# Gate table of an expert layer: matmul outputs interleaved in PSUM, eviction read straight through

## The chip, the cores and the metric

The kernel runs on one NeuronCore of a Trainium2 chip. The core has a matrix engine (TensorE, PE in the profile; its weight loads have a row of their own, PEld), a vector engine (VectorE, DVE), a scalar engine (ScalarE, ACT), GpSimd (POOL), and SyncE (SP), whose queue here only starts DMA transfers. Matmuls write PSUM, a small memory of 128 partitions with eight banks of 512 float32 values in each; ScalarE or VectorE then copy ("evict") the result into the main on-chip memory, SBUF. The metric is the device time of one execution in microseconds, the median of several runs.

## What is computed

Two layers of a transformer trunk on 512 tokens of width 1024. Each layer is an attention part (four kinds of heads) and an expert part. The expert part is the one that matters here; cut down, it reads:

```
q = (h @ w_q) ; s1, s2 = scores of 128 + 128 sub-keys, per token and head
v1,i1 = top16(s1) ; v2,i2 = top16(s2)
top_s, top_j = top16 of the 256 sums v1 + v2
eid  = i1 * 128 + i2 of the chosen pairs        # 16 of 16384 experts per head, 8 heads
gate = softmax(top_s)
act  = gelu(h . u[eid]) ; out = sum over chosen experts of gate * act * v[eid]
```

The kernel does not gather experts for the first 384 tokens. It computes the activations of all 16384 experts for them, in 128 blocks of 128, and multiplies them by a dense table of gates that is zero where an expert was not chosen. The table has, for each of the 384 tokens, 128 x 128 gates (first sub-key x second sub-key). The last 128 tokens gather their experts.

## The kernel before

`peer` (one call per layer) builds the gate table in the middle of its first stage. The table of one token is a product of two one-hot matrices, one of them scaled by the gates: 128 partitions are the token's 128 (head, choice) pairs, so a matmul sums them up.

- The table is built in 48 batches `b` of 8 tokens. `g_ones(b)` (line 1632, VectorE) makes the one-hot arrays `o` in float16 for both sub-keys. `g_scale(b, q, eng)` makes `og`, the first one-hot times the gate: `q` = 0 is the high half of the gate, `q` = 1 the rest of it, so that two float16 products carry the gate's precision. Line 1646 is its form on VectorE (one instruction for 8 tokens), line 1644 its form on ScalarE (8 instructions, one per token).
- Each batch has two groups `j` of four tokens. `g_mm(j)` (line 1654) takes a PSUM bank (tag `a`, six banks) and runs 8 matmuls of 128 columns into it: four tokens `t`, each the sum of `q` = 0 and `q` = 1. Token `t` fills columns `t*128` to `t*128+127`.
- `g_out(j)` (line 1660, ScalarE) evicts the bank of 512 columns into `gs`, a tile of 128 partitions x 128 sub-keys `a` x 32 tokens. In `gs` the tokens are innermost, so for one token neighbouring sub-keys are 32 float32 (128 bytes) apart. The eviction reads the bank straight through (token by token) and its writes step by 128 bytes.
- Eight groups fill a `gs` tile (two buffers); `g_put` (line 1663) sends its 2 MB to `gdram` in HBM from SyncE's queue.

There are 96 groups per layer, 192 in all: 1536 matmuls of line 1654 and 192 evictions of line 1660.

Beside the table run the activations of expert blocks: `u_load` (line 1343, SyncE), `u_hi` (line 1347, ScalarE) and `u_lo` (line 1350, VectorE or GpSimd) split a block of 128 x 1024 weights into two parts, `u_mm` (lines 203 to 205, tag `b`) runs 24 matmuls of 384 columns on it, `u_act` (line 1363, ScalarE) applies the gelu. VectorE also decodes the choices of the last 128 tokens (lines 1544 to 1595).

What comes in which order on each engine is decided before the program is built: `Plan` takes steps with a due time and an estimated duration (0.49 us for `g_out`, 0.45 us for `g_mm`) and writes a fixed sequence for each engine. At the end of the stage four held `u_mm` blocks run. The next stage, a loop over 128 expert blocks (`prepare`, `products`), needs the whole table: it begins with three loads of `vr` (line 1797), a load of `gq` out of `gdram` (line 1802) and six gathers (line 1750), which reuse the memory of the table's tiles.

Of the kernel before, what the change touches and what calls it, by code (L numbers as in the profile page):

```python
# [16 lines left out]
AF = mybir.ActivationFunctionType  # L17
# [25 lines left out]
GSC = 2.0 ** 14  # L43
# [1283 lines left out]
def peer(nc, tc, I, l, xd, fh, fl, h3, closing, q0, w012, both, wq_mm, right, hp, up, small, bank, mm3, iota128, pos, ident, dram, grow, ada, more, rows_out):  # L1327
    V, S, G, PE, SY = nc.vector, nc.scalar, nc.gpsimd, nc.tensor, nc.sync
# [35 lines left out]
    with tc.tile_pool(name=f"Q{l}", bufs=1) as qp:  # L1364
# [18 lines left out]
        def ac(n):  # L1383
            return "S", 0.05 + n / 1090
# [5 lines left out]
        def wq_part(h, half, eng):  # L1390

            if h not in w:
                w[h] = [q[:, :, h % 2 * 256:h % 2 * 256 + 256] for q in both]
            for k in (4 * half, 4 * half + 2):
                ks = slice(k, k + 2)
                if eng is S:
                    S.activation(w[h][0][:, ks], raw[h][:, ks], AF.Copy)
                else:
                    eng.tensor_sub(w[h][1][:, ks], raw[h][:, ks], w[h][0][:, ks])
# [10 lines left out]
        def wq_out(h, c, t=slice(0, T)):  # L1410
            if h not in qcs:
                qcs[h] = wp.tile([128, 2, T], F32, name="qc", tag="qc", bufs=3)
            S.activation(qcs[h][:, c, t], (q0[2 * h + c] if h < 2 else q1[h, c])[:, t], AF.Copy)
# [61 lines left out]
        for h in range(8):  # L1475
            t0 = 10.2 * (h - 1)
            if h > 2:
                loads[h] = plan.add(t0 - 16, lambda h=h: wq_load(h), ("Q", 3.2), take=("wr",))
                wsplit[h] = []
                for half in range(2):  # L1480
                    a = plan.add(t0 - 7 + half, lambda h=h, half=half: wq_part(h, half, S), ("S", 1.0), after=(loads[h], wtake[h] if half else None), take=("w",) if half == 0 else ())
# [5 lines left out]
            for c in range(2):  # L1487
                if h < 2:
                    m0 = plan.add(-99, none, ("none", 0), take=("a",))
                    o = plan.add(WL[0] + c, lambda h=h, c=c: wq_out(h, c, slice(0, 256)), ac(256), after=(m0, *outs), take=("qc",) if c == 0 else ())  # L1490
                    m = plan.add(WL[1] + WL[2] * (2 * (1 - h) + c), lambda h=h, c=c: wq_late(h, c), ("PE", 2.6), after=(m0, m), give=(("w", wtake[1]),) if (h, c) == (1, 1) else ())
                    late.append(plan.add(WL[1] + WL[2] * (2 * (1 - h) + c) + 2, lambda h=h, c=c: wq_out(h, c, slice(256, 512)), ac(256), after=(m, o), give=(("a", m0),)))
                else:
                    m0 = plan.add(t0 + 5.1 * c, lambda h=h, c=c: wq_half(h, c, 0), ("PE", 2.56), after=(wsplit[h][0], m), take=("a",))
                    m = plan.add(t0 + 5.1 * c + 2.5, lambda h=h, c=c: wq_half(h, c, 1), ("PE", 2.56), after=(m0, wsplit[h][1]), give=(("w", wtake[h]),) if c else ())
                    o = plan.add(t0 + 5.1 * c + 5, lambda h=h, c=c: wq_out(h, c), ac(512), after=(m, *outs), take=("qc",) if c == 0 else (), give=(("a", m0),))
# [42 lines left out]
        if True:  # L1539
# [9 lines left out]
            def ids(i, q, eng):  # L1549

                c = cids[i, q] = wp.tile([128, NC2, 8], I16, name="cid", tag="cid", bufs=2)
                o = 0
                for k0, n, wd in SELB[q]:
                    shp = [128, n, wd, 8]
                    eng.tensor_tensor(out=c[:, o:o + n * wd].rearrange("p (a b) h -> p a b h", a=n), in0=bc(ifl[:, 1, i, None, 0:wd], shp),
                                      in1=bc(ifl[:, 0, i, k0:k0 + n, None], shp), op=ALU.add)
                    o += n * wd
# [67 lines left out]
            gst, gps, oo, gg = {}, {}, {}, {}  # L1625
# [22 lines left out]
            def g_mm(j):  # L1648
                b, g = divmod(j, 2)
                o, h = oo[b], gg[b]  # L1650
                gps[j] = bank("a")
                for t in range(4):
                    for q in range(2):
                        PE.matmul(gps[j][:, t * 128:(t + 1) * 128], lhsT=o[:, 2 * g + 1, :, t], rhs=h[:, q, g, :, t], start=q == 0, stop=q == 1)  # L1654

            def g_out(j):
                tg, t4 = divmod(j, TG // 4)
                if t4 == 0:
                    gst[tg] = dp.tile([128, 128, TG], F32, name="gs", tag="gs", bufs=GL[4])
                S.activation(gst[tg][:, :, 4 * t4:4 * t4 + 4].rearrange("p a t -> p t a"), gps.pop(j).rearrange("p (t a) -> p t a", t=4), AF.Copy, scale=1 / GSC)  # L1660

            def g_put(tg):
                SY.dma_start(gdram[tg], gst.pop(tg))
# [2 lines left out]
            turns, a, f = [], None, None  # L1666
            for i in range(NT):
# [4 lines left out]
                for q in range(4):  # L1672
                    a = plan.add(due + d * q, lambda e, i=i, q=q: ids(i, q, E[e]), [("G", 0.2 * len(SELB[q]) + NSEL[q] / 60), ("W", 0.08 * len(SELB[q]) + NSEL[q] / 240)],
                                 after=(head, a), take=("cid",))
# [12 lines left out]
            for b in range(NG // 2):  # L1687
                due, (ids_, gts) = B0 + GD[0] + GD[1] * b, turns[b // 16]
                one = plan.add(due, lambda b=b: g_ones(b), ("W", 1.135), after=(ids_,), take=("o",))
                hi = plan.add(due + 1, lambda e, b=b: g_scale(b, 0, E[e]), [("W", 0.602), ("S", 2.4)], after=(one, gts), take=("og",))  # L1690
                lo = plan.add(due + 1, lambda e, b=b: g_scale(b, 1, E[e]), [("W", 0.602), ("G", 2.3), ("S", 2.4)][:LA], after=(hi,))
                for j in (2 * b, 2 * b + 1):
                    give = (("o", one), ("og", hi)) if j % 2 else ()
                    m = plan.add(due + 2, lambda j=j: g_mm(j), ("PE", 0.45), after=(lo, m if j % 2 else None), take=("a",), give=give)
                    outs.append(plan.add(due + 3, lambda j=j: g_out(j), ("S", 0.49), after=(m, *outs[:1]), take=("gs",) if j % 8 == 0 else (), give=(("a", m),)))
                if b % 4 == 3:
                    plan.add(due + 3, lambda b=b: g_put(b // 4), ("Q", 6.5), after=outs, give=(("gs", outs[0]),))
                    outs = []
# [91 lines left out]
    with tc.tile_pool(name=f"D{l}", bufs=1) as dp, ExitStack() as order:  # L1790
# [136 lines left out]
        with tc.tile_pool(name=f"X{l}", bufs=1) as xp:  # L1927
# [6 lines left out]
            def evac(i):  # L1934
                if i < 3:
                    half_out(i, 0)
                    half_out(i, 1)
                if state is not None:
                    SY.dma_start(xd[i], xs[i])
                r = put(i, xs[i], xp)  # L1940
                if state is None:
                    return r
                r[0]()
                return r[1:]
# [11 lines left out]
            if state is None:  # L1956
                scale, rest = evac(3)
                for i in range(2):
# [4 lines left out]
                    scale, rest = nxt  # L1963
# [152 lines left out]
```

## Time and profile before

| | us |
|---|---|
| median of 3 runs | 3342.16 (3340.18 to 3348.39) |
| the profiled execution | 3341.59 |
| its span, first to last instruction | 3339.8 |
| PE busy in the span | 3183.5 (95%) |
| DVE busy | 2585.4 (77%) |
| ACT busy | 1516.9 (45%) |
| line 1660, 192 evictions | 194.9 on ACT, 1144 ns each |
| line 1654, 1536 matmuls | 204.2 on PE, 295 ns each from start to end |

The table stage lies at about 522 to 720 us for the first layer and 2171 to 2368 us for the second. "Busy" of PE counts a matmul from its start to the end of its last write, and neighbouring matmuls overlap; how fast they follow each other is read from the start of the first and the start of the next, or from a run of many of them. The same holds for ScalarE: an eviction's row says 1144 ns, but the next one starts before it has ended.

### The profile page before, as it was taken

To read this page: it belongs to the slowest core of one execution; us is meant where nothing else is said; L and a number is where in the kernel's file an instruction comes from. 1 tells how busy PE (TensorE), PEld (TensorE's weight loads), DVE (VectorE), ACT (ScalarE), POOL (GpSimd) and SP (SyncE) were. 2 spreads that over 40 slices of the span, in tenths; PEclk is the share of its full clock that TensorE was granted. 3 is DMA by queue.
4 is the path that set the end of the run, shared out by engine and by line. 5 is a ranking of instruction groups with operands and counts; after the bars stand their busy time and mean duration, and the time that the engine had idled before them with its cause. 6 is when DMAs were issued, how large, how long until landed. Compare 5 with 4: busy or idle time off the path is not lost.

```text
span 3339.8 us, 48260 instructions
## 1 busy us (share of the span) xinstructions
PE 3183.5 (95%) x17540; PEld 2816.0 (84%) x17540; DVE 2585.4 (77%) x5528; ACT 1516.9 (45%) x2763; POOL 851.9 (26%) x682
## 2 busy tenths in 40 slices
PE   6999999979999999999999999998899999999998
PEld 6876879869989999998888668897799899999987
DVE  7767798858878888786666868988578787878856
ACT  3267527873333333333432864289533333333333
POOL 1300210004433343341022002100234344444400
PEclk9999999869999999999999999997899999999999
DMA  8402304459889989896654032144688899999954
GB/s 281 145 9 95 128 33 152 177 217 334 324 323 336 347 322 335 323 352 232 201 177 142 1 133 103 51 163 184 255 316 328 311 336 321 326 325 325 323 183 163
DMA packets 291343, 762.77 MB, mean 228 GB/s; under 512 B 23832, under 2 KB 130968, under 8 KB 285984
## 3 DMA queue, kind: packets, MB, share of 16 engines
q1 hardware_dynamic: 217376, 491.22, 42.3%
q0 software_dynamic: 73728, 268.47, 21.8%
q8 instruction: 137, 2.24, 0.3%
q14 instruction: 102, 0.84, 0.1%
HBM read 700.86 MB, written 58.74 MB: 227 GB/s over the span
## 4 chain that ended last, share of the span: by engine, by line
PE 75%; DVE 11%; ACT 8%; DMA 4%; issue 2%; POOL 0%; SPq 0%; DVEq 0%; ACTq 0%; POOLq 0%
PE psa L204 12%; PE psa L205 12%; PE psa L203 12%; PE psb L203 10%; PE psb L205 9%; PE psb L204 9%; ACT gs L1660 3%; PE psa L1654 2%; ACT og L1644 2%; PE psa L863 2%; PE psa L896 1%; DMA gq<-gdram 1%; DVE s L1437 1%; DMA wr<-in_w_in 1%; ACT P L877 1%
## 5 line engine op out<-in xcount | busy, mean ns | idle before, releaser
L203 PE MATMUL psb<-bh,uh 128*128 128x384 f32 x2048 | 692.0, 338 | 3.0 <-ACT act L1363 1.2
L205 PE MATMUL psb<-bh,ul 128*128 128x384 f32 x2048 | 688.9, 336 | 3.0 <-DVE ul L1350 3.0
L204 PE MATMUL psb<-bl,uh 128*128 128x384 f32 x2048 | 687.4, 336 | 0.0
L203 PE MATMUL psa<-vh,wdh 128*128 128x512 f32 x1512 | 590.8, 391 | 16.5 <-ACT wdh L1815 16.5
L205 PE MATMUL psa<-vh,wdl 128*128 128x512 f32 x1512 | 594.1, 393 | 0.0
L204 PE MATMUL psa<-vl,wdh 128*128 128x512 f32 x1512 | 593.8, 393 | 0.0
L1750 POOL DMA_INDIRECT gt<-in_peer_u,eid x256 | 341.6, 1334 | 726.3 <-DVE gt L1770 233.7
L1815 ACT ACTIVATE wdh<-act 128x384 fp32r<-128x384 f32 x252 | 132.1, 524 | 862.2 <-PE psa L204 640.6
L1750 POOL DMA_INDIRECT gt<-in_peer_v,eid x256 | 322.7, 1261 | 425.3 <-DVE a L1775 195.7
L203 PEld LDWEIGHTS psb<-bh,uh 128*128 128x128 f32 x2048 | 386.6, 189 | 13.2 <-DVE arow L250 2.6
L204 PEld LDWEIGHTS psb<-bl,uh 128*128 128x128 f32 x2048 | 386.1, 189 | 7.3
L205 PEld LDWEIGHTS psb<-bh,ul 128*128 128x128 f32 x2048 | 385.5, 188 | 4.7 <-DVE ul L1350 4.3
L1350 DVE TENSOR_TENSOR ul<-ur,uh 128x1024 fp32r<-128x1024 f32 x246 | 301.6, 1226 | 100.1 <-ACT uh L1347 87.8
L1816 DVE TENSOR_TENSOR wdl<-act,wdh 128x384 fp32r<-128x384 f32 x252 | 140.9, 559 | 286.6 <-ACT wdh L1815 272.1
L203 PEld LDWEIGHTS psa<-vh,wdh 128*128 128x128 f32 x1512 | 285.3, 189 | 72.2 <-ACT wdh L1815 17.1
L205 PEld LDWEIGHTS psa<-vh,wdl 128*128 128x128 f32 x1512 | 285.0, 188 | 60.1
L1827 DVE TENSOR_TENSOR vl<-vr,vh 128x1024 fp32r<-128x1024 f32 x252 | 307.8, 1221 | 33.0 <-ACT vh L1824 22.7
L204 PEld LDWEIGHTS psa<-vl,wdh 128*128 128x128 f32 x1512 | 285.1, 189 | 56.1
L1775 DVE SCALAR_TENSOR_TENSOR a<-gt,w,a 128x1024 f32<-128x1024 f32 x254 | 325.6, 1282 | 0.8
L1770 DVE SCALAR_TENSOR_TENSOR gt<-gt,h 128x1024 f32<-128x1024 f32 x256 | 310.9, 1220 | 0.0
L1347 ACT ACTIVATE uh<-ur 128x1024 fp32r<-128x1024 f32 x256 | 268.4, 1049 | 76.0 <-PE psb L204 64.2
L1363 ACT ACTIVATE act<-psb 128x384 f32<-128x384 f32 x256 | 126.8, 495 | 340.3 <-PE psb L205 340.2
(387 smaller groups left out, 5374.2 us busy)
## 6 DMA issues: line engine op xcount, KB each, us to landing
ur<-in_peer_uT SPq DMA_DIRECT2D x256, 512.0 KB
vr<-in_peer_v SPq DMA_DIRECT2D x256, 512.0 KB
gdram<-gs SPq DMA_DIRECT2D x24, 2048.0 KB
gq<-gdram SPq DMA_DIRECT2D x64, 768.0 KB
O<-in_ada_w SPq DMA_DIRECT2D x48, 512.0 KB
gt<-in_ada_w SPq DMA_DIRECT2D x32, 512.0 KB
wr<-in_w_q SPq DMA_DIRECT2D x14, 1024.0 KB
wr<-in_w_out SPq DMA_DIRECT2D x16, 512.0 KB
```

The lines of the kernel that those rows point to most:

```text
L203: PE.matmul(ps, lhsT=wh, rhs=mh, start=first, stop=False)
L204: PE.matmul(ps, lhsT=wh, rhs=ml, start=False, stop=False)
L205: PE.matmul(ps, lhsT=wl, rhs=mh, start=False, stop=last)
L1347: S.activation(uspl[e][0], uraw[e], AF.Copy)
L1350: eng.tensor_sub(uspl[e][1], uraw.pop(e), uspl[e][0])
L1363: S.activation(acts[e], ups.pop(e)[:, :384], AF.Gelu_apprx_tanh)
L1750: G.indirect_dma_start(out=t, out_offset=None, in_=I["peer_u" if kind == "u" else "peer_v"], in_offset=bass.IndirectOffsetOnAxis(ap=eid3[: ...
L1770: V.scalar_tensor_tensor(t, t, 1.0, h3, op0=ALU.mult, op1=ALU.mult, accum_out=d3[:, s:s + 1])
L1775: V.scalar_tensor_tensor(a3, t, w3[:, s:s + 1], a3, op0=ALU.mult, op1=ALU.add)
L1815: S.activation(wh, w, AF.Copy)
L1816: V.tensor_sub(wl, w, wh)
L1827: V.tensor_sub(vspl[e][1], vraw.pop(e), vspl[e][0])
```

## The change

The matmuls of token `t` now write columns `t`, `t+4`, `t+8` and so on of the bank: four float32 (16 bytes) from one column to the next, so that the four tokens of one sub-key lie side by side. The eviction reads the bank straight through as before, but now in the order sub-key, token, and writes runs of four tokens (16 bytes); the next run starts 128 bytes further on. `gs`, `gdram` and everything behind them are the same.

```
     gps[j] = bank("a")
     for t in range(4):
         for q in range(2):
-            PE.matmul(gps[j][:, t * 128:(t + 1) * 128], lhsT=o[:, 2 * g + 1, :, t], rhs=h[:, q, g, :, t], start=q == 0, stop=q == 1)
+            PE.matmul(gps[j].rearrange("p (a t) -> p a t", t=4)[:, :, t], lhsT=o[:, 2 * g + 1, :, t], rhs=h[:, q, g, :, t], start=q == 0, stop=q == 1)
...
-    S.activation(gst[tg][:, :, 4 * t4:4 * t4 + 4].rearrange("p a t -> p t a"), gps.pop(j).rearrange("p (t a) -> p t a", t=4), AF.Copy, scale=1 / GSC)
+    S.activation(gst[tg][:, :, 4 * t4:4 * t4 + 4], gps.pop(j).rearrange("p (a t) -> p a t", t=4), AF.Copy, scale=1 / GSC)
```

The estimates of the planner are not touched. The sequence of instructions on every engine and what each of them waits for stay as they are; the evictions and the table's matmuls alone have other access patterns. The number of instructions and of elements is the same.

## Rows read from the trace of the kernel before

**Rows 1.** The page: busy time by engine, then the chain that ended last.
```profile
PE 3183.5 (95%) x17540; PEld 2816.0 (84%) x17540; DVE 2585.4 (77%) x5528; ACT 1516.9 (45%) x2763; POOL 851.9 (26%) x682
...
PE 75%; DVE 11%; ACT 8%; DMA 4%; issue 2%; POOL 0%; SPq 0%; DVEq 0%; ACTq 0%; POOLq 0%
```
**Rows 2.** Windows, busy us: PE, PEld, DVE, ACT, POOL, TensorE clock, DMA share, GB/s.
```profile
580.00:600.00 20.00, 20.00 (x134) 19.44 (x134) 15.18 (x31) 15.04 (x24) 0.00 (x0) 1.00 0.51 184
620.00:640.00 20.00, 20.00 (x138) 19.58 (x138) 16.59 (x30) 19.34 (x34) 2.90 (x1) 1.00 0.48 183
645.80:719.98 74.18, 55.64 (x389) 46.53 (x387) 57.66 (x90) 74.17 (x146) 0.00 (x0) 0.59 0.42 174
658.49:707.47 48.98, 35.28 (x256) 29.28 (x256) 39.24 (x61) 48.98 (x98) 0.00 (x0) 0.60 0.41 172
2293.60:2367.60 74.00, 55.49 (x393) 46.52 (x393) 57.52 (x90) 74.00 (x146) 0.00 (x0) 0.62 0.42 172
```
**Rows 3.** Timeline, one cycle of the table: start us, us, engine, line, tiles, count.
```profile
658.49 2.66 ACT L1644 ACTIVATE og<-o,gL 128x128 f16<-128x128 f16 x8
...
659.07 4.42 PE L1654 MATMUL psa<-og,o 128*128 128x128 f16 x32 [1.90 <-ACT og L1644]
...
660.89 3.90 ACT L1660 ACTIVATE gs<-psa 128x512 f32<-128x512 f32 x4
661.51 0.69 DVE L1646 TENSOR_TENSOR og<-o,gT 128x1024 f16<-128x1024 f16 x1 [1.43 <-PE psa L1654]
...
664.60 2.66 ACT L1644 ACTIVATE og<-o,gL 128x128 f16<-128x128 f16 x8
```
**Rows 4.** Waits, 658.49 to 707.47 us: who waited for whom, us in total, times, longest.
```profile
PE psa L1654 <- ACT og L1644: 13.9, 8, 1.9
DVE og L1646 <- PE psa L1654: 9.2, 8, 1.4
```
**Rows 5.** Timeline of ScalarE: four evictions that write 128x512 without steps.
```profile
307.53 2.07 ACT L802 ACTIVATE PT<-psa 128x512 f32<-128x512 f32 x4 [0.19 <-PE psa L896]
```
**Rows 6.** Groups of ScalarE: line, tiles, shape, count, busy us, mean ns.
```profile
L1660 ACT ACTIVATE gs<-psa 128x512 f32<-128x512 f32 x192 | 194.9, 1144 | 6.4 <-PE psa L1654 5.0
...
L802 ACT ACTIVATE PT<-psa 128x512 f32<-128x512 f32 x68 | 38.8, 590 | 7.3 <-PE psa L896 7.1
```
**Rows 7.** Windows of line 1654 alone: PE and PEld busy us, TensorE clock, DMA, GB/s.
```profile
574.30:577.00 2.70, 2.70 (x23) 2.65 (x24) 1.00 0.00 0
673.70:675.60 1.90, 1.90 (x18) 1.85 (x16) 0.50 1.07 457
```
**Rows 8.** Timeline of the weight loads: line 1654 at full clock, then `u_mm` at half clock.
```profile
574.30 2.71 PEld L1654 LDWEIGHTS <-o 128*128 128x128 f16 x24 [0.16 <-issue]
...
716.24 0.33 PEld L203 LDWEIGHTS psb<-bh,uh 128*128 128x128 f32 x1
716.56 0.33 PEld L204 LDWEIGHTS psb<-bl,uh 128*128 128x128 f32 x1
```
**Rows 9.** Chain by time: matmuls of 256 columns at full clock; start us, us, what.
```profile
145.10 0.12 PE psa L203
145.22 0.12 PE psa L204
145.34 0.12 PE psa L205
145.46 0.11 PE psa L203
```
**Rows 10.** Groups, 645 to 720 us: the table's matmuls.
```profile
L1654 PE MATMUL psa<-og,o 128*128 128x128 f16 x377 | 52.4, 292 | 18.5 <-ACT og L1644 18.0 <-DVE og L1646 0.5
```
**Rows 11.** Chain by time, after the first layer's last eviction.
```profile
720.00 6.99 DMA gdram<-gs
...
728.40 16.84 DMA gq<-gdram
745.27 0.57 DVE act L1806
```

## The prediction

> **What bounds the kernel now.** I read the page first: PE is busy 95% of the span, and the chain that ended last is 75% PE and only 8% ACT [rows 1]. So an eviction on ScalarE that becomes cheaper gains nothing over most of the span, and the question is where those 8% lie. The windows answer it. From 580 to 640 us PE is busy in every microsecond, while ACT has room [rows 2]: there the table's matmuls lie between those of the expert blocks, and the evictions hide. From 645.8 us to the last eviction at 720 us it is the other way round: ACT is busy 74.17 of 74.18 us, PE 55.64, DVE 57.66; the second layer has the same stretch, 74.00 of 74.00 us [rows 2]. So there are two stretches of 74 us in which ScalarE alone sets the pace. After each comes a fixed tail: the last piece of the table goes to HBM in 7 us, the next stage's first load out of it takes 17 us, and then its first VectorE step starts [rows 11]. These transfers start when the table is done, so the rest of the layer moves with the table's end, microsecond for microsecond.
>
> Inside a stretch the work repeats, and the timeline shows one cycle [rows 3]: 8 scaling steps on ACT, 32 matmuls that follow them, four evictions, then the next 8 scaling steps, 6.11 us after the first. Eight such cycles fill 658.49 to 707.47 us, 6.12 us each, with ACT busy throughout [rows 2]. In them PE waits 13.9 us for ACT's scaling, and DVE waits 9.2 us for PE to release an `og` buffer [rows 4].
>
> **The eviction.** Four of them take 3.90 us in the timeline, the last with its full length of about 1.13 us, so one starts 0.92 us after the other [rows 3]. Four evictions of the same 128 x 512 values that write without steps take 2.07 us; with 0.59 us for the last, their pace is 0.49 us [rows 5, 6]. Both read PSUM straight through; the difference of 0.43 us is the writes that step 128 bytes at every one of 512 values. Bounds for the new form, which steps at every fourth value: 0.49 us if runs of four cost nothing, 0.60 us if every step left keeps its price (a quarter of 0.43 us on top), and 0.92 us if a short run is as bad as a single value. Scaling steps are a hint towards the low end: line 1644 reads and writes every fourth 2-byte value, two of them in 16 bytes, and 8 of them start within 2.4 us (660.89 less 658.49), 0.30 us each for 128 values [rows 3], so steps within 16 bytes hardly slow ScalarE. I take 0.5 to 0.6. [...]
>
> **The matmuls.** This is the part that no row shows: none of the kernel's matmuls writes PSUM in steps. [...] Yet a column costs twice the time at half clock: `u_mm` with 384 columns takes 0.32 us there, 0.83 ns a column [rows 8], so 128 columns stream in about 0.107 us at half clock and 0.053 us at full clock. [...] Matmuls of 256 columns at full clock stream as long, and follow each other in 0.11 to 0.12 us, each with a weight load of 128 columns [rows 9]. So at full clock every table matmul has some 0.055 us in hand behind its weight load. If a step of 16 bytes doubles the time of a column from 0.42 to 0.83 ns, the pace stays at 0.12 us and nothing is lost; if it costs more, 1536 matmuls get longer, 768 a layer. The lower bound is the pace of today (a gain is excluded, since the weight load sets that pace), the upper one the doubling of the slow column: 1.67 ns, 0.213 us for 128, with the 0.012 us that the pace has on top today 0.225 us. I take the lower, since the nearest rows are those of half clock and of 256 columns, and in both a column or a matmul of twice the time is covered.
>
> **The sum for one layer.** ACT's part of a cycle falls from 6.12 us to 2.46 us of scaling plus four evictions of 0.49 to 0.60: 4.4 to 4.9 us. PE's part is 32 matmuls of 0.12, 3.9 us. DVE is late next: 48.98 us less the 9.2 us of waiting leaves 39.8 us of work, 4.97 us a cycle [rows 2, 4]. The loop between the engines is shorter: from ACT's scaling at 658.49 to DVE's next `og` at 661.51, 0.69 us more for that, so ACT could scale again after 3.8 us [rows 3]. I take 5.1 us for the new cycle, DVE's 4.97 and a little waiting: 1.02 us saved, eight times, 8.2 us. The irregular ends of the stretch (645.8 to 658.5 and 707.5 to 720 us, 12.6 us each) hold eight evictions each; ACT alone would give back 8 x 0.43 = 3.4 us at each, but DVE and PE hand over less evenly there, and I take 4.5 us for both. Before 645 us PE is full and I take 0.5 us. That is 13.2 us a layer, 26.4 us for two. The `gs` buffers do not bound it: a put lands in 7 us [rows 11], and two cycles fill a tile in 10.
>
> The profiled execution took 3341.59 us, 0.57 below the median. 3341.59 - 26.4 = 3315.2, and on the median's scale 3315.8; I say 3315. Own range of this case: an eviction pace of 0.70 makes ACT's cycle 5.26 us, 10 us a layer, 3322; a matmul a tenth slower costs PE's full stretch (391 of 768 matmuls, the rest being the 377 of [rows 10]) 4.7 us a layer, 3325; and if DVE were no bound, ACT's cycle of 4.42 us would give 1.7 x 8 + 6.8 = 20.4 us a layer, 3301. So 3300 to 3330.
>
> **Rivals.**
>
> 1. *Steps in PSUM slow the matmuls beyond their cover.* The mechanism is the column rate: at 0.225 us a matmul, the 391 matmuls of the stretch in which PE is full cost 391 x 0.105 = 41 us a layer. In ScalarE's stretch 377 x 0.225 is 85 us, with the expert matmuls at its end some 89, against 74 now: 15 more, less some 6 us of early waits that it fills. About 50 a layer, 100 in all: 3440. The point from which it decides: an excess of x us a matmul costs 391x before 645 us, against 13 us gained, so a pace of about 0.15 us loses the whole gain, and 0.16 us ends some 12 us above it. For it speaks that the margin is thin (0.107 in 0.12) and that PE has no other room from 560 to 640 us; against it, that [rows 9] shows a stream of that length covered. [...]
>
> 2. *The eviction stays as slow.* If a run of 16 bytes costs as much as single values, ACT keeps its 6.12 us and nothing moves: 3342. Against it stand [rows 5] and the scaling steps.
>
> 3. *The gain is taken back.* The table ends earlier, but the load of `gq`, the gathers and three `vr` loads still share the DMA engines. They start only with the table's end, so I expect them to move as a block; if the held expert blocks then finish late, some microseconds of 26 go. This lies within the forecast's own range.
>
> **How the numbers follow.** Forecast 3315, chance 0.66, with 3300 to 3330 for itself. Rival 1 at its full price (3440) 0.15; in between, a pace of 0.155 to 0.19 us (3345 to 3390), 0.08. No change, by rival 2 or by a pace near 0.15 that eats the gain, 0.11. What this kernel's measurement tells from no change is about 0.3%, 10 us. Faster by more: 0.67; within: 0.11; slower: 0.22. To leave out no more than two in ten, the range must take in no change and the smaller half of the in-between cases: 3300 to 3370.
>
> **What would show it.** Line 1660 at about 600 ns in place of 1144, and a pace near 0.5 us. Line 1654's runs of 24 still in 2.7 to 2.9 us at full clock: this is the step on which all hangs, and runs of 5 us there would prove rival 1. Two stretches of 60 to 61 us in place of 74, with ACT no longer full and DVE busy over nine tenths of it; the load of `gq` starting about 13 us earlier in the first layer and 26 us in the second. I am wrong if the PE stretch from 560 to 645 us gets longer, or if the stretch shrinks and the next stage still starts where it did.

## The result, and the profile of the changed kernel

The changed kernel takes 3303.78 us (median of 4 runs, 3296.51 to 3308.73), the kernel before 3341.47 us beside it: a ratio of 0.9881, with a 95% interval of 0.9855 to 0.9907. Measured a second time later it took 3308.40 us (5 runs, 3305.73 to 3309.47) against 3342.51 us, a ratio of 0.9903 (0.9886 to 0.9919). So the gain is 34 to 38 us; forecast were 26, for a time of 3315 us. The profiled execution took 3308.73 us with a span of 3307.0 us, 32.9 us less than that of before.

The page, as in [rows 1]: busy time by engine, then the chain that ended last.

```profile
PE 3173.3 (96%) x17540; PEld 2813.7 (85%) x17540; DVE 2582.4 (78%) x5528; ACT 1442.8 (44%) x2763; POOL 847.2 (26%) x682
...
PE 76%; DVE 14%; DMA 4%; ACT 3%; issue 2%; POOL 0%; SPq 0%; DVEq 0%; POOLq 0%; ACTq 0%
```

Every engine runs as many instructions as before, and only ACT has clearly less to do, 74 us. Of the chain ACT had 8% and has 3%; 3 of these 5 points went to DVE. That is the change of bound in one line: the wait that ends last in the two stretches is now one for VectorE.

The windows, as in [rows 2]: two of the time in which TensorE is full, then the two stretches from the same matmul group as before to the last eviction, and between them the eight cycles of the first.

```profile
580.00:600.00 20.00, 20.00 (x135) 19.46 (x134) 15.01 (x31) 11.26 (x22) 0.00 (x0) 1.00 0.50 171
620.00:640.00 20.00, 20.00 (x139) 19.57 (x136) 16.76 (x33) 16.07 (x34) 2.89 (x1) 1.00 0.48 180
645.55:704.92 59.37, 48.88 (x375) 42.38 (x373) 56.29 (x89) 55.06 (x145) 0.00 (x0) 1.00 0.51 213
654.37:693.98 39.61, 32.68 (x255) 28.68 (x254) 37.27 (x59) 37.00 (x98) 0.00 (x0) 1.00 0.51 213
2275.74:2335.13 59.39, 48.91 (x375) 42.39 (x373) 56.31 (x89) 55.07 (x145) 0.00 (x0) 1.00 0.52 213
```

Where TensorE is full, 20 us hold 135 and 139 matmuls, against 134 and 138 in [rows 2]: it lost nothing there. The sign that the prediction named for it, a run of 24 weight loads of line 1654 at full clock (granted 1.00), reads 2.70 and 2.71 us, against 2.71 in [rows 8]:

```profile
567.02 2.70 PEld L1654 LDWEIGHTS <-o 128*128 128x128 f16 x24 [0.16 <-issue]
...
574.05 2.71 PEld L1654 LDWEIGHTS <-o 128*128 128x128 f16 x24 [0.16 <-issue]
```

The stretches take 59.4 us instead of 74; ACT is busy 93% of them, DVE 95%. Eight cycles take 39.61 us instead of 48.98: 4.95 us each instead of 6.12. One figure stands out that no step of the prediction asked for: TensorE's granted clock in the stretches is 1.00, and was 0.59 to 0.62.

The timeline of one cycle (start us, us, engine, line), as in [rows 3]:

```profile
654.37 2.71 ACT L1644 ACTIVATE og<-o,gL 128x128 f16<-128x128 f16 x8
...
656.80 2.13 ACT L1660 ACTIVATE gs<-psa 128x512 f32<-128x512 f32 x4
657.17 0.68 DVE L1646 TENSOR_TENSOR og<-o,gT 128x1024 f16<-128x1024 f16 x1
657.77 0.64 DVE L1555 TENSOR_TENSOR cid<-ifl 128x96 int16<-128x96 int16 x6
657.90 0.15 PEld L1654 LDWEIGHTS <-o 128*128 128x128 f16 x2 [0.31 <-DVE og L1646]
658.32 1.29 DVE L1646 TENSOR_TENSOR og<-o,gT 128x1024 f16<-128x1024 f16 x2
...
659.06 1.70 PE L1654 MATMUL psa<-og,o 128*128 128x128 f16 x13 [0.85 <-DVE og L1646]
```

Four evictions that took 3.90 us take 2.13. Behind them PE waits 0.85 us for DVE's `og`, where in [rows 3] it waited 1.90 us for ACT's; DVE had first done six small steps of the token lists (`cid`). The waits of the eight cycles (who waited for whom, us in total, times, longest) say the same beside [rows 4], where PE's 13.9 us went to ACT:

```profile
PE psa L1654 <- DVE og L1646: 6.5, 7, 1.3
...
ACT gs L1660 <- PE psa L1654: 2.3, 7, 0.3
DVE o L1632 <- PE psa L1654: 2.3, 8, 0.3
```

One eviction has a median of 598 ns (min, median, max here; first and last start), the mean in [rows 6] was 1144:

```profile
L1660 ACT ACTIVATE gs<-psa x192: 565/598/714, 530.5 to 2334.5; 128x512 f32<-128x512 f32 x192
```

The tail after the first layer's last eviction at 704.92 us, by the chain (start us, us, what), answers to [rows 11]:

```profile
712.61 18.49 DMA gq<-gdram
731.12 0.57 DVE act L1806
```

The load starts 15.8 us earlier than before and takes 1.65 us longer; the step behind it starts 14.2 us earlier. In the second layer that step starts at 2360.69 us, before at 2393.44: 32.8 us earlier, practically the whole difference of the two executions.

### The profile page after: what moved, and what is told of

Its sections match the earlier page's. It is cut to its first block, busy times and chain, and to the rows that moved or that the text cites. A ratio compares the mean times of both kernels' runs of the same rounds, so it can differ in the third digit from the quotient of the medians.

```text
span 3307.0 us, 48260 instructions
## 1 busy us (share of the span) xinstructions
PE 3173.3 (96%) x17540; PEld 2813.7 (85%) x17540; DVE 2582.4 (78%) x5528; ACT 1442.8 (44%) x2763; POOL 847.2 (26%) x682
## 4 chain that ended last, share of the span: by engine, by line
PE 76%; DVE 14%; DMA 4%; ACT 3%; issue 2%; POOL 0%; SPq 0%; DVEq 0%; POOLq 0%; ACTq 0%
PE psa L204 12%; PE psa L205 12%; PE psa L203 12%; PE psb L203 10%; PE psb L205 10%; PE psb L204 10%; PE psa L1654 4%; PE psa L863 2%; DVE o L1632 1%; DMA gq<-gdram 1%; PE psa L896 1%; DVE s L1437 1%; DMA wr<-in_w_in 1%; DVE og L1646 1%; ACT P L877 1%
```

## The experiments

Two questions were open: which half of the change brings the gain, and whether the stepped matmuls are free because a slower column is covered, or because a step costs nothing at all. Then: what bounds the stretch now. One measure serves most of the runs: from the start of the table's first matmul in a layer to the start of its last one. The list of line 1654's instructions gives it for each layer. It repeats within 0.1 us in the two layers of most kernels, while the whole time has runs several us apart (the kernel before and the eviction alone have layers that differ by TensorE's granted clock ahead of the stretch, as will be seen). Each ratio is taken against the kernel before on the same chip (3338.88 to 3342.51 us).

| kernel | layer 1, us | layer 2, us | time, us (runs) | ratio to before, 95% |
| --- | --- | --- | --- | --- |
| before | 189.8 | 187.3 | 3341.47 (4) | 1 |
| matmuls stepped alone | 187.3 | 187.3 | 3336.77 (10) | 0.9987 (0.9970 to 1.0003) |
| eviction alone | 176.7 | 176.7 | 3308.94 (4) | 0.9897 (0.9864 to 0.9929) |
| eviction alone, again | 176.8 | 175.3 | 3307.29 (5) | 0.9898 (0.9881 to 0.9915) |
| changed kernel | 175.3 | 175.3 | 3303.78 (4) | 0.9881 (0.9855 to 0.9907) |
| changed kernel, again | 175.2 | 175.3 | 3308.40 (5) | 0.9903 (0.9886 to 0.9919) |
| two VectorE copies more, changed | 183.4 | 182.4 | 3320.23 (4) | 0.9940 (0.9923 to 0.9956) |
| two VectorE copies more, before | 190.4 | 190.7 | 3344.43 (10) | 1.0012 (1.0000 to 1.0024) |
| each eviction twice, changed | 199.8 | 199.8 | 3370.39 (1) | no interval |
| planner's price raised, `ids` on VectorE, changed | 167.6 | 167.7 | 3287.09 (5) | 0.9841 (0.9823 to 0.9860) |

**The matmuls alone.** The eviction still writes steps of 128 bytes:

```
-  PE.matmul(gps[j][:, t * 128:(t + 1) * 128], ...
+  PE.matmul(gps[j].rearrange("p (a t) -> p a t", t=4)[:, :, t], ...
-  S.activation(gst...rearrange("p a t -> p t a"), gps.pop(j).rearrange("p (t a) -> p t a", t=4), ...
+  S.activation(gst...rearrange("p a t -> p t a"), gps.pop(j).rearrange("p (a t) -> p t a", t=4), ...
```

> The matmuls' half of the change alone: they write PSUM in steps of four columns, and the eviction reads it back in those steps, token by token, and writes by 128 bytes as before. Theory (the whole gain is the eviction's writes, the steps cost TensorE nothing here): evictions start 0.92 us apart, matmuls of the table 0.12 us apart, time as before, 3341 us within 8. Rival 1 (the matmul steps bring a gain themselves): near 3304 us. Rival 2 (reading PSUM in steps costs ScalarE on top of the stepped writes): evictions about 1.3 us apart, ScalarE's stretches 12 evictions longer by 5 us each, above 3370 us.

Timeline of ScalarE, then a window (columns as above):

```profile
659.42 3.94 ACT L1660 ACTIVATE gs<-psa 128x512 f32<-128x512 f32 x4
```
```profile
660.00:680.00 20.00, 17.09 (x114) 14.58 (x113) 15.70 (x20) 20.00 (x39) 0.00 (x0) 0.89 0.39 166
```

Four evictions take 3.94 us and ACT is full, as in [rows 3]; the time has no measurable difference from before. The stepped matmuls therefore do not bring the gain, and they cost nothing that the time can tell (by the interval between 10 us less and 1 us more). What this kernel's slow eviction shares with the one of before is the write of single values 128 bytes apart.

**The eviction alone.** Matmuls as before; the eviction reads PSUM in steps of 512 bytes and writes runs of four. Its timeline of ScalarE and a window follow the expectation:

```
-  S.activation(gst...rearrange("p a t -> p t a"), gps.pop(j).rearrange("p (t a) -> p t a", t=4), ...
+  S.activation(gst[tg][:, :, 4 * t4:4 * t4 + 4], gps.pop(j).rearrange("p (t a) -> p a t", t=4), ...
```

> The eviction's half alone: matmuls write the bank token by token as before, the eviction reads it in steps of 128 columns (512 bytes) and writes runs of four tokens. Theory (writes into SBUF set the old pace, reads of PSUM in steps are free for ScalarE): evictions 0.49 us apart, 3304 us within 10, as the full change. Rival (ScalarE reads in steps as slowly as it writes in steps): 0.92 us apart, 3341 us; then the matmuls' half is what makes the gain possible.

```profile
650.90 3.56 ACT L1660 ACTIVATE gs<-psa 128x512 f32<-128x512 f32 x7
```
```profile
660.00:680.00 20.00, 16.40 (x130) 14.61 (x128) 18.86 (x31) 18.95 (x52) 0.00 (x0) 0.63 0.50 211
```

Seven evictions in 3.56 us: less the last one's 0.60 that is 0.49 us each, the full pace, though PSUM is read in steps of 512 bytes. DVE and ACT are as busy as in the changed kernel, and the time is its time. So half of the change would have done: ScalarE reading PSUM in steps of 512 bytes was as fast here as reading it straight (seven evictions in 3.56 us in the changed kernel as well).

The first measurements put the changed kernel 5 us below this one, and its stretch ran at a granted clock of 1.00 instead of 0.63. That made a second theory: the steps bring a few us by way of the clock. Both kernels were run again, side by side.

> The changed kernel, unaltered, beside the next run, to weigh the stepped matmuls by themselves. Theory (the whole gain is ScalarE's shorter write; a stepped column costs nothing at 128 columns; TensorE's clock in the two stretches is granted 1.00 instead of 0.60 and gives back a few us in the matmuls that need their columns): 3304, 3300 to 3309, that is 4 to 6 us below the next run. Rival (the steps of the matmuls do nothing at all, and the 5 us seen between single measurements were scatter): equal to the next run within 2 us.

> Matmuls as before, the eviction alone turned round: it reads PSUM in steps of 512 bytes and writes runs of four. Theory: 3309, 3306 to 3313, with a granted clock of 0.60 to 0.66 in the stretch of 640 to 700 us. Rival: 3304, the same as the changed kernel, whatever its clock.

The window of 660 to 680 us, first of the changed kernel, then of the eviction alone:

```profile
660.00:680.00 20.00, 16.57 (x131) 14.55 (x130) 18.87 (x30) 19.37 (x53) 0.00 (x0) 1.00 0.56 236
```
```profile
660.00:680.00 20.00, 16.54 (x131) 14.65 (x128) 18.85 (x30) 19.16 (x50) 0.00 (x0) 0.67 0.56 236
```

The clocks differ again, 1.00 and 0.67, and the times do not: 3308.40 and 3307.29 us. The second theory fell: the 5 us did not come back. The layers of the eviction alone (second measurement) show where the clock counts and where it does not; for each layer, the time from the table's first matmul to the stretch, then the stretch:

```profile
529.59:647.93 118.34, 116.86 (x792) 113.20 (x792) 97.94 (x169) 85.35 (x174) 5.74 (x2) 0.98 0.47 169
647.93:707.27 59.34, 48.79 (x373) 42.98 (x372) 56.30 (x89) 55.06 (x145) 0.00 (x0) 0.64 0.52 213
2157.56:2274.40 116.84, 115.32 (x791) 111.65 (x791) 97.91 (x169) 85.40 (x174) 5.72 (x2) 1.00 0.47 172
2274.40:2333.77 59.37, 48.82 (x373) 42.90 (x372) 56.31 (x89) 55.06 (x145) 0.00 (x0) 0.68 0.52 213
```

The stretch takes 59.3 to 59.4 us at 0.64 and 0.68, and 59.4 in the changed kernel at 1.00: there the clock gives nothing back. The 1.4 us by which this kernel lies behind in the table come from the time ahead of the stretch, in which TensorE is full, and only where the granted clock fell there (118.3 us at 0.98 against 116.8 at 1.00). Its second layer, without such a fall, needs 175.3 us like the changed kernel.

**What a step costs a matmul.** At 128 columns a cost could hide behind the weight load, so it was measured where nothing hides it. Four matmuls of 512 columns take the place of a group's eight in the changed kernel, first straight, then in steps of four columns; both leave out the table's real content:

```
-  for t in range(4):
+  for t in range(2):
-  PE.matmul(gps[j].rearrange("p (a t) -> p a t", t=4)[:, :, t], lhsT=o[:, 2 * g + 1, :, t], rhs=h[:, q, g, :, t], ...
+  PE.matmul(gps[j], lhsT=o[:, 2 * g + 1, :, t], rhs=h[:, q, g].rearrange("p c t -> p (c t)"), ...
```

In steps of four columns, the same line reads:

```
+  PE.matmul(gps[j].rearrange("p (a s) -> p s a", s=4), lhsT=o[:, 2 * g + 1, :, t], rhs=h[:, q, g].rearrange("p c t -> p (c t)").rearrange("p (s a) -> p s a", s=4), ...
```

> Measures the disputed cost, first half: the table's 8 matmuls of 128 columns a group are replaced by 4 of 512 columns, written without steps (the table is then not the reference's). Both theories: 0.22 us from one to the next at the full clock, 4 of them 0.88 us against 0.95 us now, time near that of the changed kernel, 3290 to 3310 us.

> Second half: the same 4 matmuls of 512 columns, their output in steps of four columns. Theory (a step doubles the time of a column at full clock, and in the changed kernel this hides behind the weight load): 0.43 us from one to the next, 0.84 us more a group, 192 groups 161 us, less some 25 us a layer of TensorE's idle time: about 3410 us. Rival A (steps cost TensorE nothing at all): 0.22 us, time as the run without steps. Rival B (the doubled slow column of the prediction's first rival): 0.86 us apart and 3700 us or more.

Chain by time, straight and then in steps of four columns:

```profile
563.34 2.62 PE psa L1654 x12
```
```profile
577.27 5.18 PE psa L1654 x12
```

2.62 us for 12 are 0.218 us a matmul, 0.43 ns a column; in steps 0.432 us, 0.84 ns a column, both at a granted clock of 1.00. The time went from 3295.54 to 3415.13 us (one run each). So a step of 16 bytes is not free and not four times: it doubles the column. By that a stepped matmul of 128 columns needs an estimated 0.108 us for its columns, and one table matmul follows the other after 0.113 to 0.117 us anyway (24 weight loads in 2.70 us in the changed kernel; the median of a load is 117 ns).

A further kernel used steps of two columns, 8 bytes, to see whether the price goes by the size of the step.

> Four matmuls of 512 columns a group in place of eight of 128, their output in steps of two columns (8 bytes) in place of four (16 bytes); it leaves the table's real content out. Theory D (any step breaks up PSUM's writes, and the price is two column times, as with four): 0.43 us a matmul, about 3415. Rival E (only a step of more than 8 bytes costs): 0.22 us, about 3295 as without steps. Rival F (price by the step): something between, 0.3 us, 3340 to 3360.

```profile
574.70 5.18 PE psa L1654 x12
```

Again 5.18 us for 12, and 3413.10 us in all: the price is the same double at 8 and at 16 bytes. At 512 columns a step costs a factor of two here (0.432 us at either step, 0.218 without), and at 128 columns behind a weight load nothing (24 in 2.70 and 2.71 us, 2.71 without steps). Why a step doubles the time was not shown.

**VectorE as the next bound.** Two copies of 128x128 were put on VectorE for every batch of the table, in the changed kernel and in that of before:

```
+  V.tensor_copy(vpad, iota128)
+  V.tensor_copy(vpad, iota128)
```

> The changed kernel with two small VectorE copies (128 x 128 float32) added to every batch, about 0.3 us a batch. Theory (VectorE is the next bound in the two stretches): some 24 batches of each stretch move the end by their whole time, 7 us a layer: 3316 us, 3311 to 3322. Rival (ScalarE or the hand-over between engines is the bound): within 3 us of the changed kernel, 3304.

> The same two copies in the kernel before. Theory: VectorE waits 9.2 us in eight cycles there, 0.57 us a batch, and takes 0.3 us for nothing: 3342 us, within 4. Rival (VectorE is a bound in both kernels): 7 us a layer, 3356 us.

The window 640 to 700 us of the changed kernel with the copies:

```profile
640.00:700.00 60.00, 47.56 (x350) 41.59 (x350) 57.43 (x127) 51.74 (x126) 0.00 (x0) 0.97 0.47 193
```

By the ratios the same copies cost the changed kernel 12 to 20 us (0.9940 against 0.9903 and 0.9881), and that of before 4 us, with an interval that reaches to nothing. DVE is busy 57.43 of 60 us and ACT falls to 51.74. In the kernel of before, the first layer's stretch is no longer with the copies than without, 73.88 us against 74.2, and ACT stays full:

```profile
648.07:721.95 73.88, 55.68 (x395) 46.50 (x394) 64.49 (x133) 73.88 (x146) 0.00 (x0) 0.62 0.41 171
```

What it lost lies ahead of the stretch (121.1 and 121.4 us in the two layers, against 120.2 and 117.7). VectorE bounds the stretch now, and did not before.

**The eviction twice.** The reverse test: give ScalarE its length back.

```
+  for _ in range(2):
+      S.activation(gst[tg][:, :, 4 * t4:4 * t4 + 4], gps[j].rearrange("p (a t) -> p a t", t=4), ...
```

> The changed kernel with every eviction run twice into the same place, about 0.98 us a group in place of 0.49. Theory (the gain is ScalarE's time and nothing else; the matmul steps are free): ScalarE sets the pace again, a cycle of 2.46 + 3.9 = 6.4 us, time 3342 to 3352 us, at or a little above the kernel before. Rival (the gain comes from the other access patterns, not from ScalarE's time): stays near 3304.

```profile
667.55 2.65 ACT L1644 ACTIVATE og<-o,gL 128x128 f16<-128x128 f16 x8
669.95 4.67 ACT L1661 ACTIVATE gs<-psa 128x512 f32<-128x512 f32 x8
674.51 2.70 ACT L1644 ACTIVATE og<-o,gL 128x128 f16<-128x128 f16 x8
```

The direction held and the size did not: 3370.39 us, 18 us above the upper end of what was expected. Eight evictions take 4.67 us, 0.58 us from one to the next on average instead of 0.49, and the cycle is 6.96 us (674.51 less 667.55), longer than the 6.12 of before. From the first of the eight to the next scaling step it is 4.56 us (674.51 less 669.95) where 3.9 were expected, which covers what 6.96 has over the expected 6.4. Why evictions run twice into the same place follow each other more slowly was not shown. The run shows at least that ACT's length sets the time again as soon as it is the longest.

**A version that uses the room.** The order of this kernel comes from a planner with a price for each step. The matmul group is priced at 0.45 us, though eight matmuls of 0.12 us take 0.95. The price was set to that, and the `ids` step was tied to VectorE, where the planner may otherwise put it on GpSimd:

```
-  ids(...), [("G", 0.2 * len(SELB[q]) + NSEL[q] / 60), ("W", 0.08 * len(SELB[q]) + NSEL[q] / 240)]
+  ids(...), [("W", 0.08 * len(SELB[q]) + NSEL[q] / 240)]
-  m = plan.add(due + 2, lambda j=j: g_mm(j), ("PE", 0.45), ...
+  m = plan.add(due + 2, lambda j=j: g_mm(j), ("PE", 0.95), ...
```

> The changed kernel, with the planner's estimate of a group's matmuls set to the 0.95 us that the trace shows (0.45 before), and the sums of sub-key numbers kept on VectorE. Theory: with true prices the planner spreads expert matmuls and table matmuls better, so that TensorE is idle less in the last stretch; VectorE is near its bound there, so 0 to 10 us a layer: 3285 to 3304 us. Rival (order does not matter, VectorE bounds the whole stage): 3304 within 5.

> The changed kernel with the planner's price of a matmul group raised from 0.45 to 0.95 us and the `ids` step kept on VectorE alone, so that the planner spreads the work as the shorter eviction allows. Theory (after the change no engine is full alone, and the order sets the rest): 3291, 3286 to 3297, ScalarE full again between 640 and 680 us and VectorE under 19 of 20. Rival (its one earlier time was luck): 3304 as the changed kernel.

Second measurement: two windows, then ScalarE's timeline.

```profile
640.00:660.00 20.00, 17.56 (x142) 16.00 (x141) 18.87 (x25) 20.00 (x55) 0.00 (x0) 1.00 0.53 224
660.00:680.00 20.00, 17.95 (x149) 16.96 (x147) 18.56 (x23) 20.00 (x57) 0.00 (x0) 1.00 0.63 264
```
```profile
663.86 2.77 ACT L1644 ACTIVATE og<-o,gL 128x128 f16<-128x128 f16 x8
666.32 2.19 ACT L1660 ACTIVATE gs<-psa 128x512 f32<-128x512 f32 x4
668.33 2.78 ACT L1644 ACTIVATE og<-o,gL 128x128 f16<-128x128 f16 x8
```

3290.75 us in one run and 3287.09 in five, 0.9841 of before: faster than both kernels. The cycle is 4.47 us (668.33 less 663.86) and ACT is full from 640 to 680 us, so this is ScalarE's own length: 2.46 us of scaling (666.32 less 663.86) and 2.01 us for four evictions (668.33 less 666.32). In the 20 us from 660 VectorE does 23 steps here, all of them `o` and `og`, and 30 in the changed kernel: none of its small steps stands between them. Which of the two edits does it was not tested apart.

## Why the prediction was right

- **The bound.** Two stretches in which ACT alone sets the pace, with a tail that moves with their end: right. The tail moved as a block, 15.8 us at its start in layer 1 (about 13 expected) and 32.8 us in layer 2 (26 expected). Of rival 3 there is a trace, the 1.65 us by which the first load of `gq` got longer.
- **The eviction.** 0.49 us was the low end of three bounds, and the four evictions in 2.07 us of [rows 5] were the right row to go by. Writing runs of four values, seven evictions took 3.56 us, 0.49 us from one to the next, as the straight writes of [rows 5]. The prediction's second argument, the scaling steps, proves little, since no row has them without steps. A run of two values was not measured. Rival 2 fell.
- **The matmuls.** The step on which all hung was argued from half the clock and from 256 columns: a column of twice the time is covered. Half the clock shows it by [rows 7, 8]: 24 weight loads of line 1654 take 2.71 us at a granted clock of 1.00 and 16 take 1.85 us at 0.50, 0.113 and 0.116 us each, and 128 columns at 0.50 need an estimated 0.107 us (384 of them follow each other in 0.32 us). That is what happened. The runs with 512 columns show the doubling (2.62 us for 12 matmuls, 5.18 in steps), and the runs of 24 (2.70 and 2.71 us) and the windows at 580 and 620 us (135 and 139 matmuls, 134 and 138 before) show it covered. That the price would be no more than a doubling stood in no row, as the prediction says: this half was a bet that came in. Rival 1 needed more than a doubling and fell. One of its sums does not come out: with its pace of 0.12 us, 0.16 us would cost 391 x 0.04 = 15.6 us a layer against 13 gained, which ends 5 us above no change in two layers and not 12. Nothing hangs on it.
- **The sum was too small**, 26.4 us against 32.9 between the two profiles. From the first matmul of the table to its last eviction, before and after (525.6 to 719.98 and 528.7 to 704.92 us; 2175.6 to 2367.60 and 2158.9 to 2335.13), the stage lost 18.2 us in layer 1 and 15.8 in layer 2, each against 13.2; the rest of the span took 1.1 us more. From one and the same matmul group on, the stretch gave 14.8 and 14.9 us, where the sum has 12.7 (8.2 for the cycles, 4.5 for the ends). The time ahead of it gave 3.4 and 0.9 us in place of 0.5.
- **The ends of the stretch were the term mis-sized.** The windows of the same 60 instructions of VectorE, from one `o` to the one of 16 batches later, before and then after (the count of 61 has one that reaches over the edge):

```profile
657.09:706.23 49.14, 35.28 (x257) 29.28 (x256) 39.41 (x60) 49.14 (x97) 0.00 (x0) 0.60 0.41 172
```
```profile
656.02:696.97 40.95, 33.01 (x258) 29.01 (x257) 38.60 (x61) 38.34 (x101) 0.00 (x0) 1.00 0.53 222
```

  That is 6.14 and 5.12 us a cycle, 8.2 us in eight, as forecast. In part this is luck: a cycle has 4.83 us of VectorE's work and 0.29 of waiting, where the sum had 4.97 and 0.13. It had taken everything but the one wait for work (39.8 us, though the row shows 39.24 busy). What is left of the stretch went from 25.0 to 18.4 us: the ends gave 6.6 us, almost the 6.8 that ACT alone would give back, and the sum had cut that to 4.5. Most of it, 5.8 us, lies behind these cycles: to the last eviction it is 13.75 us before and 7.95 after. Cut at ScalarE's scaling steps instead, as in [rows 2] and the windows above, eight cycles give 9.4 us and the ends 5.4; but these two windows hold 25 and 23 `og` steps of VectorE, so they are not the same work.
- **Why layer 1 gave 2.5 us more ahead of the stretch.** The windows of 543 to 561 us, before and then after:

```profile
543.00:561.00 18.00, 16.91 (x101) 16.21 (x99) 14.44 (x19) 17.64 (x36) 0.00 (x0) 0.81 0.55 223
```
```profile
543.00:561.00 18.00, 17.48 (x127) 16.88 (x126) 15.45 (x19) 14.90 (x36) 0.00 (x0) 1.00 0.56 220
```

  In the profile of before, TensorE waited for ACT until 555.29 us, and the expert matmuls behind that followed each other in 0.32 us, as in [rows 8] at half clock, where those of the changed kernel take 0.17: 101 matmuls in the window in place of 127. The kernel with stepped matmuls alone needed 187.3 us in layer 1 as well, where before needed 189.8, at a granted clock of 1.00 in that window. So this part came with the clock, and the prediction's sum had no term for it. Whether it belongs to the change is open. Of the kernel before one layer of two has such a fall, of the eviction alone three of four have a smaller one (0.98 over the time ahead of the stretch, 1.5 us), of the stepped matmuls alone and of the changed kernel none.

## What to carry to other kernels

An eviction that scatters single float32 values over SBUF, 0.92 us from one to the next, was made as fast as a straight one, 0.49 us, by letting it write runs of four. The turning round could stand on the read side, where ScalarE's steps of 512 bytes in PSUM cost nothing (0.49 us); the producer need not have changed. If a matmul does write in steps, compare twice its column time, as measured here, with the pace that its weight load sets. At 128 columns it stayed below that pace (an estimated 0.108 us against 0.113 to 0.117) and the steps were free; at 512 columns it lay above, and they doubled the matmul (0.218 to 0.432 us). After such an edit the next bound decides what arrives, and where a planner sets the order, its prices may have to be set anew: with the `ids` step tied to VectorE as well, that gave some 13 to 21 us (by the ratios) on top of the 34 to 38.

## What the runs showed of the hardware beyond that

- TensorE's granted clock differs between kernels whose rows of TensorE otherwise read alike. In the window of 660 to 680 us it was 0.63 and 0.67 with straight columns and 1.00 with stepped ones, each with about 16.5 us busy and 130 matmuls. With ACT as slow as before it was 0.59 straight and 0.89 stepped in that window. In the stretch it was worth nothing (59.3 to 59.4 us at 0.64, 0.68 and 1.00), since the table's matmuls keep their pace at either level (24 weight loads in 2.71 us at 1.00, 16 in 1.85 us at 0.50, [rows 7, 8]) and VectorE, busy 56.3 of these 59.4 us, sets the time. Ahead of it, where TensorE is full, a granted clock of 0.98 instead of 1.00 cost 1.5 us (118.3 against 116.8). Why more is granted was not tested.
- A column written to PSUM in steps takes twice as long at 8 and at 16 bytes (0.432 us for 512 in place of 0.218).
